# Two-layer hybrid backbone: convolutions issued behind their columns, sums taken from PSUM, first maxima among the last gates, and several loads and tiles moved

## The chip, the cores and the metric

The kernel runs on one core of a Trainium2 chip. A core has TensorE (PE, matrix products, with its weight loads shown as PEld), VectorE (DVE), ScalarE (ACT), GpSimd (POOL) and SyncE (SP, which here only issues transfers). Each engine works through its own queue in order. Transfers (DMA) are issued by SP, ACT or POOL and move data between the memory of the chip and the core's SBUF, by 16 DMA engines. The metric is the device time of one execution in microseconds (us); lower is better.

## The reference, cut to what matters

2048 latent tokens of width 1024, with 256 context tokens, go through two layers. Each layer: RMS norm, modulation by a condition (adaLN), one wide input projection, two mixers side by side, each multiplied by its own SiLU gate, one output projection, and a residual through the modulation's gate. The mixers of the first layer are global grouped attention (8 query heads, 2 key heads, rotary, QK norm) and a Hyena long convolution of order 2; those of the second are windowed attention with a sink and a two-dimensional neighbourhood attention. In short:

```python
# first layer
y_a = global_gqa(q, k, v, k_c, v_c)
y_b = hyena_branch(hu, conv_w, ..., d_skip)
y = jnp.concatenate([y_a * jax.nn.silu(ag), y_b * jax.nn.silu(hg)], axis=-1)
# second layer: windowed_gqa(...) and neighbourhood_attention(...)
# both: x = x + gate * (y @ w_out)
```

Everything is float32.

## The kernel before, in words

**Products.** A float32 operand is split into a high and a low part, and a product is three matmuls (hi*hi, hi*lo, lo*hi; `mm3`, printed in the profile as L221). Weights come as pieces of 256 KB (`wraw`, L241), ACT casts the high part (L242), POOL takes the difference (L243).

**Order.** Blocks of instructions are written in program order, and a planner of the framework places them on the engines by its own simulated times, earlier program order going first when two are ready. Within an engine and within a DMA queue the order is then fixed. Only the matmuls inside the global attention are kept in the order in which they are written (`manual_schedule` for PE). Tiles come from rings of a few buffers; a new tile waits for the last use of the buffer that it takes. Pools that are closed give their place to later pools, so a tile of a new pool can wait for the old pool's last use.

**First layer.** Tokens go in three groups `GRP[0..2]`. For each group: norm, rows of k, v, q (PSUM tile `psA`), columns of `u` for Hyena (`us`, PSUM tile `psB`, stored to `u0`), columns of the gates (`g0`). Between them stand the context's attention and Hyena, and the modulation for the gates and for the second layer: `ada_sum` (L95) adds over weights that are loaded in steps into three PSUM banks of the pool `xp`, tag "x"; transposes (L103) end it. For the last group the order is `us((0, 1)); conv(0); us((2,)); conv(1)`, where `conv(0)` and `conv(1)` are the two parts of `latent_conv`: short convolution on DVE and ACT, transposes, and for part 0 the first transform stage (`hpA`, L668, which uses PSUM tag "x" too). Then come the gate columns, `gate_convs`, the rows of k, v, q, and the last gate columns with the maxima.

**First maxima.** For the softmax the global attention takes a maximum of each query's scores: per unit (4 query blocks x 4 head pairs = 16 units) 40 steps of one matmul `pm` (L892) and one reduction `mx` (L893). Those of the first unit (`first_maxima`, `M0`) run ahead of the attention: `cols` calls `some_maxima` after each of four pairs of columns, seven steps at a time, and 12 steps follow. `max_fin` turns the maxima into a row `mr`, which ACT's queue sends into Q (L945).

**Global attention (`glob_attn`).** 144 batches of two key tiles: scores `pS` (L979, L980), exponential on ACT (`Pt`, L981), values `po` (L998), sums of `Pt` on POOL (`pacc`, L993), and the maxima of the next unit in between (`upto`). `load_k` and `load_q` fetch K and Q. Into the batches `hooks(b)` puts the Hyena steps (110 batches, `hyena_steps`; the first transform's matrix `dA` is loaded by `first_stage`, L661, and cast by ACT, L664), then `out_pools`, then from batch 125 on the first output jobs. A unit's end is `finish` (reciprocal, gate, `finish_y`, which stores the result to `yT` as high and low parts).

**Output jobs (`out_jobs`).** A job takes one tile of 128 tokens and one half of the output columns: weights, the two tiles `oy` of `yT` (L1401), the tile `ox` of x or ctx (L1419), `mm3` into `pso`, the product with the gate (L1425) and the sum with x (L1426). After the attention follow, for each group, residual statistics, norm (transposes `lnpt` L302, `lnh` L305 on ACT), rows and columns of the second layer. In the last group `window_keys` loads the keys and values of the window attention (L1452 to L1454) after the q rows of that attention.

## Time and profile before

| what | value |
|---|---|
| median of 3 runs | 3856.79 us (3853.07 to 3857.14) |
| the profiled execution | 3855.73 us |
| its span | 3854.0 us, 57179 instructions |
| mean granted TensorE clock | 0.975 of 2.4 GHz |
| busy: PE, DVE, ACT, POOL | 94%, 59%, 46%, 45% of the span |
| DMA | 586.23 MB, 152 GB/s over the span |

The span is the time from the first to the last instruction in the trace. "Idle before" in a row is the time in which the engine stood still before that instruction, and the arrow names what ended it. A row's time of start counts from the span's start.

### The profile page before, as it was taken

The page shows a single profiled execution, that of the slowest core. Times are in us where ns is not written, and L with a number is a line of the kernel's source. Part 1 is how long each engine was busy: PE and PEld are TensorE (multiplying, and loading weights), DVE is VectorE, ACT ScalarE, POOL GpSimd, SP SyncE. Part 2 cuts the span into 40 slices and gives each one's busy share as a digit, 9 for nine tenths or more (in the row PEclk, how much of TensorE's full clock was granted, in tenths as well). Part 3 has the DMA queues.
Part 4 walks back from the last instruction along what each step waited for, and adds up shares of the span by engine and source line. Part 5 has one row for each costly group of instructions (what it writes and reads, how often), then busy time and mean ns, then how long its engine had stood idle before and what let it go on. Part 6 is the DMA issues. An engine that isn't in the chain of part 4 may idle for free.

```text
span 3854.0 us, 57179 instructions
## 1 busy us (share of the span) xinstructions
PE 3628.1 (94%) x20112; PEld 2607.1 (68%) x20112; DVE 2284.9 (59%) x4370; ACT 1784.9 (46%) x3480; POOL 1735.3 (45%) x1433
## 2 busy tenths in 40 slices
PE   6999999999779999999989989999999999999999
PEld 2788777666555544555545667778877888888887
DVE  5854862634967765776664348185168167677622
ACT  3644642423526655666452334344144266666610
POOL 1544642222447786777796554353244123222310
PEclk8999999999889999999999999999999999999999
DMA  6343445366666555443253545545566376365365
GB/s 195 118 140 123 133 133 141 114 224 219 203 191 189 172 162 173 123 148 110 91 197 96 146 148 152 164 152 155 157 175 169 118 171 147 90 151 135 113 178 169
DMA packets 537650, 586.23 MB, mean 152 GB/s; under 512 B 70590, under 2 KB 361720, under 8 KB 534290
## 3 DMA queue, kind: packets, MB, share of 16 engines
q1 hardware_dynamic: 521090, 551.10, 48.8%
q10 hardware_dynamic: 13856, 25.18, 1.8%
q0 software_dynamic: 2416, 6.29, 0.6%
q8 instruction: 159, 2.61, 0.3%
q14 instruction: 129, 1.06, 0.1%
HBM read 389.62 MB, written 192.75 MB: 151 GB/s over the span
## 4 chain that ended last, share of the span: by engine, by line
PE 69%; DVE 13%; issue 5%; DMA 5%; ACT 4%; POOL 2%; SPq 1%; ACTq 0%; DVEq 0%; POOLq 0%
PE psB L221 16%; PE pso L221 7%; PE po L998 6%; PE psA L221 5%; PE npt L1580 4%; PE no L1592 4%; PE pS L979 4%; PE pm L892 3%; PE pS L980 3%; PE ns L1561 2%; PE ns L1567 2%; DMA wraw<-in_w_in_dram 2%; PE hpX L806 1%; PE hpC L799 1%; PE hpH L811 1%
## 5 line engine op out<-in xcount | busy, mean ns | idle before, releaser
L243 POOL TENSOR_TENSOR wlo<-wraw,whi 128x512 fp32r<-128x512 f32 x368 | 494.4, 1357 | 784.9 <-ACT whi L242 529.3
L993 POOL TENSOR_TENSOR pacc<-pacc,Pt 128x512 f32<-128x512 f32 x512 | 647.1, 1286 | 191.4 <-ACT Pt L981 189.1
L221 PE MATMUL psB<-hT,whi 128*128 128x512 f32 (+1 forms) x2560 | 659.4, 346 | 3.9 <-DVE bo L341 3.5
L221 PE MATMUL psA<-whi,hT 128*128 128x512 f32 (+1 forms) x1952 | 574.8, 375 | 28.3 <-ACT vt L361 8.4
L893 DVE TENSOR_REDUCE mx<-pm 128x1 f32<-128x512 f32 (+1 forms) x640 | 389.1, 631 | 194.4 <-PE pm L892 190.1
L221 PEld LDWEIGHTS psB<-hT,whi 128*128 128x128 f32 x2560 | 445.1, 190 | 87.0 <-issue 23.9
L981 ACT ACTIVATE Pt<-pS 128x512 f32<-128x512 f32 x576 | 333.0, 597 | 352.5 <-PE pS L980 313.7
L221 PE MATMUL psB<-hT,wlo 128*128 128x512 f32 (+1 forms) x1280 | 433.8, 344 | 0.0
L221 PEld LDWEIGHTS psA<-whi,hT 128*128 128x128 f32 x1952 | 359.0, 194 | 98.7 <-ACT vt L361 11.7
L242 ACT CAST whi<-wraw 128x512 fp32r<-128x512 f32 x368 | 222.2, 618 | 301.4 <-DMA wraw<-in_w_in_dram 119.5
L221 PE MATMUL psA<-wlo,hT 128*128 128x512 f32 (+1 forms) x976 | 358.3, 372 | 0.9 <-POOL wlo L243 0.8
L221 PE MATMUL pso<-whi,oy 128*128 128x512 f32 x1088 | 343.2, 394 | 7.9 <-DMA oy<-yT 7.0
L979 PE MATMUL pS<-Q,K 128*128 128x512 f32 x576 | 330.9, 574 | 15.3 <-ACT Pt L981 14.9
L998 PE MATMUL po<-Pt,V 128*64 128x512 f32 x1152 | 283.0, 613 | 0.0
L221 PEld LDWEIGHTS psB<-hT,wlo 128*128 128x128 f32 x1280 | 242.4, 190 | 41.1 <-issue 10.8
L1580 PE MATMUL npt<-ident,np 128*128 128x128 f32 x1488 | 258.6, 283 | 3.4 <-DVE ggt L1157 1.9
L979 PEld LDWEIGHTS pS<-Q,K 128*128 128x128 f32 x576 | 109.7, 190 | 208.7 <-issue 95.3
L221 PEld LDWEIGHTS pso<-whi,oy 128*128 128x128 f32 x1088 | 205.2, 189 | 59.0 <-DMA oy<-yT 7.0
L980 PE MATMUL pS<-Q,K 65*128 65x512 f32 x576 | 231.3, 402 | 10.9 <-DMA Q<-mr 10.9
L892 PE MATMUL pm<-K,Q 128*128 128x512 f32 x600 | 217.0, 384 | 16.6 <-DVE mx L893 16.5
L221 PE MATMUL pso<-wlo,oy 128*128 128x512 f32 x544 | 213.2, 394 | 1.2 <-POOL wlo L243 1.2
L221 PEld LDWEIGHTS psA<-wlo,hT 128*128 128x128 f32 x976 | 189.9, 195 | 32.4 <-POOL wlo L243 3.1
(345 smaller groups left out, 6490.8 us busy)
## 6 DMA issues: line engine op xcount, KB each, us to landing
wraw<-in_w_in_dram SPq DMA_DIRECT2D x312, 256.0 KB
oy<-yT SPq DMA_DIRECT2D x72, 512.0 KB
qk<-tq SPq DMA_DIRECT2D x50, 512.0 KB
fA<-fev SPq DMA_DIRECT2D x64, 256.0 KB
adaw<-in_w_ada_dram SPq DMA_DIRECT2D x32, 512.0 KB
hxb<-XA SPq DMA_DIRECT2D x64, 256.0 KB
hfb<-fA SPq DMA_DIRECT2D x64, 256.0 KB
XC<-hevc ACTq DMA_DIRECT2D x64, 256.0 KB
```

Of the source, the lines that this page charges most:

```text
L221: T.matmul(ps, a(x, kt), b(y, kt), start=(kt == 0 and n == 0), stop=(kt == 7 and n == 2))
L242: S.copy(hi, w)
L243: G.tensor_tensor(out=lo, in0=w, in1=hi.bitcast(F32), op=ALU.subtract)
L892: T.matmul(pm[:, :n], self.q1[:, h, qt * P:(qt + 1) * P], self.K1(c0, n), start=True, stop=True)
L893: V.tensor_reduce(out=self.mx[:, u, c:c + 1], in_=pm[:, :n], axis=AX.X, op=ALU.max)
L979: T.matmul(s, K1[kv][:, kt * P:(kt + 1) * P], q1[:, h, :], start=True, stop=False)
L980: T.matmul(s, K2[kv][:, kt * P:(kt + 1) * P], q2[:, h, :], start=False, stop=True)
L981: S.activation(pt[:, h, :], s, AF.Exp)
L993: G.tensor_tensor(out=acc[1][:, h], in0=acc[1][:, h], in1=p[:, h], op=ALU.add)
L998: T.matmul(po[64 * h:64 * h + 64, :], vt[:, kt, kv * 64:kv * 64 + 64], p[:, h, :], start=(kt == 0), stop=(kt == 17))
L1580: T.transpose(pt[:, i, :], self.p[h][:, (i0 + i) * P:(i0 + i + 1) * P], ident)
L1592: T.matmul(B["po"][64 * h:64 * h + 64, self.k, :], vt[:, kt, 64 * h:64 * h + 64], self.pT[h, i // 4][:, i % 4, :], start=(i == 0), stop=(i ...
```

## The change

It has eight parts. (1) `us((0,)); conv(0); us((1,)); conv(1); us((2,))` in place of the order above. (2) The 40 maxima of the first unit are called 12, 12, 8 and 8 at a time after the four pairs of the last gate columns, and none after them. (3) `load_k` fetches the first key head in two chunks of columns, 0 to 512 and 512 to 2304. (4) The first transform's matrix of the Hyena steps is loaded at the step `o == 0, k2 == 20`, behind a one-column copy on DVE from that step's tile. (5) In an output job the loads of `oy` stand ahead of the weights; in group 0 the load of x from the third tile on waits for a one-column copy from the x tile two jobs before; the product with the gate is written back to PSUM, and the sum takes it from there. (6) The tiles of the last attention unit's end lie in the ring of `oy` (`last_home`). (7) `window_keys` is called after the v rows of the neighbourhood attention, its loads behind one-column copies from the last v tile. (8) `ev_v` keeps its last tile for that.

```diff
--- before.py
+++ after.py
@@ -347,7 +347,7 @@
 
         def ev_v(self, dst):
             def f(ps, tt):
-                vt = self.rg.tile([P, 512], F32, tag="bo", name="vt", bufs=3)
+                vt = self.late = self.rg.tile([P, 512], F32, tag="bo", name="vt", bufs=3)
                 S.copy(vt, ps)
                 nc.sync.dma_start(dst[tt], vt)
             return f
@@ -362,10 +362,10 @@
                 nc.sync.dma_start(dv[tt], vt)
             return f
 
-    def finish_y(sb, y, ft, t0, n, yT=yT, tags=("yhi", "ylo"), bufs=2, eng=None):
-
-        hi = sb.tile([P, 512], F32R, tag=tags[0], name="yhi", bufs=bufs)
-        lo = sb.tile([P, 512], F32R, tag=tags[1], name="ylo", bufs=bufs)
+    def finish_y(sb, y, ft, t0, n, yT=yT, tags=("yhi", "ylo"), bufs=2, eng=None, home=None):
+
+        hi = home[0] if home else sb.tile([P, 512], F32R, tag=tags[0], name="yhi", bufs=bufs)
+        lo = home[1] if home else sb.tile([P, 512], F32R, tag=tags[1], name="ylo", bufs=bufs)
         S.copy(hi[:, :n], y)
         (eng or V).tensor_tensor(out=lo[:, :n], in0=y, in1=hi[:, :n].bitcast(F32), op=ALU.subtract)
         nc.sync.dma_start(yT[0, ft, :, t0:t0 + n], hi[:, :n].bitcast(F32))
@@ -655,9 +655,11 @@
             V.tensor_tensor(out=y, in0=pt.rearrange("p a b -> p (a b)")[:, :256], in1=gt, op=ALU.mult)
             finish_y(sb, y, 4 + ct, 2048, 256, tags=("cmX", "cmt"), bufs=1)
 
-    def first_stage(sb):
+    def first_stage(sb, late=None):
 
         dA = sb.tile([P, P], F32, tag="dA", name="dA")
+        if late is not None:
+            V.tensor_copy(dA[:, 0:1], late[:, 0:1])
         nc.sync.dma_start(dA, C['dftA'])
         hi = sb.tile([P, P], F32R, tag="dAh", name="dAh")
         lo = sb.tile([P, P], F32R, tag="dAl", name="dAl")
@@ -754,7 +756,6 @@
     def hyena_steps(sb, ps):
 
 
-        dA = first_stage(sb)[1]
         dD = sb.tile([P, 64], F32, tag="hdD", name="hdD")
         nc.sync.dma_start(dD, C['dftD'])
         yb = sb.tile([P, 4, 2048], F32, tag="yb", name="yb")
@@ -765,7 +766,7 @@
 
         def stage_a(o, g, zt):
             pA = [bank("hpA") for _ in range(2)]
-            dA(pA, zt)
+            D["dA"](pA, zt)
             for h in range(2):
                 ev = sb.tile([P, 512], F32, tag="hev", name="hev", bufs=3)
                 S.copy(ev, pA[h])
@@ -799,6 +800,8 @@
             T.matmul(pC, D["dC", o, k2 // 4][:, k2 % 4, :], D.pop(("Y", o, k2)), start=True, stop=True)
             ev = sb.tile([P, 512], F32, tag="hev", name="hevc", bufs=3)
             S.copy(ev, pC)
+            if o == 0 and k2 == 20:
+                D["dA"] = first_stage(sb, ev)[1]
             nc.scalar.dma_start(XC[o, k2].rearrange("r n c -> (r n) c"), ev)
 
         def forward_x(o, k2):
@@ -904,7 +907,7 @@
                 nc.gpsimd.dma_start(ks[-1][64 * s:64 * s + 64, :n].bitcast(F32), k0[0, 0:64, c:c + n])
         return Maxima(lambda c, n: ks[c // 1024][:, c % 1024:c % 1024 + n], q1, mx, bank)
 
-    def glob_attn(sb, ps, hooks, M0):
+    def glob_attn(sb, ps, hooks, M0, last_home):
 
 
         K1, K2 = [None] * 2, [None] * 2
@@ -928,10 +931,13 @@
             return q1, q2, M
 
         def load_k(h, eng=nc.sync):
-            for s in range(2):
-                eng.dma_start(K1[h][64 * s:64 * s + 64].bitcast(F32), k0[h, 0:64, :])
-            G.memset(K2[h][64:65].bitcast(F32), 1.0)
-            eng.dma_start(K2[h][0:64].bitcast(F32), k0[h, 64:128, :])
+            for i, c in enumerate(((0, 512), (512, 2304)) if h == 0 else ((0, 2304),)):
+                c = slice(*c)
+                for s in range(2):
+                    eng.dma_start(K1[h][64 * s:64 * s + 64, c].bitcast(F32), k0[h, 0:64, c])
+                if i == 0:
+                    G.memset(K2[h][64:65].bitcast(F32), 1.0)
+                eng.dma_start(K2[h][0:64, c].bitcast(F32), k0[h, 64:128, c])
 
         def max_fin(q):
             q1, q2, mx = q[0], q[1], q[2].mx
@@ -1000,12 +1006,13 @@
         def finish(n, yo, acc):
 
             qb, hp = units[n]
-            gt = sb.tile([P, 512], F32, tag="agt", name="agt", bufs=1)
+            tail = iter(home[0]) if n == 15 else None
+            gt = next(tail) if tail else sb.tile([P, 512], F32, tag="agt", name="agt", bufs=1)
             nc.sync.dma_start(gt, g0[hp, :, qb * 512:qb * 512 + 512])
             pd = ps.tile([P, 512], F32, tag="m", name="pd", bufs=3)
             for h in range(2):
                 T.matmul(pd[64 * h:64 * h + 64, :], ones[:, 64:P], acc[:, h, :], start=True, stop=True)
-            rec = sb.tile([P, 512], F32, tag="rec", name="rec", bufs=1)
+            rec = next(tail) if tail else sb.tile([P, 512], F32, tag="rec", name="rec", bufs=1)
             S.copy(rec, pd)
 
             def quarter(i):
@@ -1015,11 +1022,12 @@
                 G.tensor_tensor(out=rec, in0=rec, in1=gt, op=ALU.mult)
                 G.tensor_tensor(out=yo, in0=yo, in1=rec, op=ALU.mult)
 
-            return [lambda i=i: quarter(i) for i in range(0, 512, 128)] + [gate, lambda: finish_y(sb, yo, hp, qb * 512, 512, bufs=1, eng=G)]
+            return [lambda i=i: quarter(i) for i in range(0, 512, 128)] + [gate, lambda: finish_y(sb, yo, hp, qb * 512, 512, bufs=1, eng=G, home=home[1] if tail else None)]
 
         batches = [(n, kt) for n in range(16) for kt in range(0, 18, 2)]
         nb = len(batches)
         acc, po, ended, last, pend = {}, {}, {}, None, []
+        home = []
         total = 16 * 41
 
         def upto(b, share):
@@ -1061,7 +1069,9 @@
                 for i in range(2):
                     values(m, ks + i, tiles[i], po[m])
                 if ks == 16:
-                    yo = sb.tile([P, 512], F32, tag="yo", name="yo", bufs=2)
+                    if m == 15:
+                        home[:] = last_home()
+                    yo = home[0].pop() if m == 15 else sb.tile([P, 512], F32, tag="yo", name="yo", bufs=2)
                     S.copy(yo, po.pop(m))
                     ended[b + 2] = m, yo
             if b in ended:
@@ -1316,7 +1326,7 @@
         xs2 = ln_in(GRP[2][0])
         gates()
         ln0(2, xs2)
-        us((0, 1))
+        us((0,))
         ls = s2.enter_context(tc.tile_pool(name="lc", bufs=1))
 
         def conv(part):
@@ -1324,8 +1334,9 @@
                         lambda: sb.tile([P, 1024], F32, tag="lnx", name="zev", bufs=6), (part,))
 
         conv(0)
+        us((1,))
+        conv(1)
         us((2,))
-        conv(1)
         s2.close()
         gates((0,))
         with ExitStack() as s2:
@@ -1334,13 +1345,13 @@
         M0 = first_maxima(lambda: sb.tile([P, 1024], F32R, tag="lnx", name="K1", bufs=6), cp.tile([P, 8, 5], F32, tag="sil", name="mx"),
                           lambda: xp.tile([P, 512], F32, tag="x", name="pm", bufs=3))
 
+        share = [12, 12, 8, 8]
+
         def some_maxima():
-            for _ in range(7):
+            for _ in range(share.pop(0)):
                 M0.step()
 
         pj.cols(2304 + 512, True, g0[4:8], True, some_maxima, (sb, "lnh", 2))
-        while M0.i < 40:
-            M0.step()
     HB = 2
     hy = stH.enter_context(tc.tile_pool(name="hy", bufs=1, **L))
     hyp = stH.enter_context(tc.tile_pool(name="hyp", bufs=1, space=PSUM, **L))
@@ -1391,14 +1402,14 @@
         def job(b, i, tt, mm):
             c = slice(512 * b, 512 * b + 512)
             rg, xo, gl = O0["rg"], O0["xo"], O0["gl"]
+            ty = [xo.tile([P, 8, P], F32R, tag=f"oy{s}", name=f"oy{s}", bufs=2) for s in range(2)]
+            for s in range(2):
+                nc.sync.dma_start(ty[s].bitcast(F32), yT[s, :, :, tt * P:(tt + 1) * P].rearrange("f p t -> p f t"))
             if i == 0 and w_out.get("b") != b:
                 w_out["b"] = b
                 w_out["w"] = load_w(I['w_out'][0][:, c], 512)
             if g == 0 and i == 0:
                 gate_half(gl[:, c], mm("pg"), 0, 0, b)
-            ty = [xo.tile([P, 8, P], F32R, tag=f"oy{s}", name=f"oy{s}", bufs=2) for s in range(2)]
-            for s in range(2):
-                nc.sync.dma_start(ty[s].bitcast(F32), yT[s, :, :, tt * P:(tt + 1) * P].rearrange("f p t -> p f t"))
             gate = gl[:, c]
             if tt == 16:
                 w_out["gc"] = rg.tile([P, 512], F32, tag="bo", name="gc", bufs=3)
@@ -1411,6 +1422,8 @@
             else:
                 if len(xs) == i:
                     xt = xo.tile([P, 1024], F32, tag="lnx", name="ox", bufs=6)
+                    if g == 0 and i > 1:
+                        V.tensor_copy(xt[:, 0:1], xs[i - 2][:, 0:1])
                     if early:
                         for h in range(2):
                             hs = slice(512 * h, 512 * h + 512)
@@ -1421,9 +1434,8 @@
                 x = xs[i][:, c]
             po = mm("pso")
             mm3((po, lambda x, kt: ty[x][:, kt, :], lambda y, kt: w_out["w"][y][kt]))
-            t = rg.tile([P, 512], F32, tag="bo", name="ot", bufs=3)
-            V.tensor_tensor(out=t, in0=po, in1=gate, op=ALU.mult)
-            V.tensor_tensor(out=x, in0=x, in1=t, op=ALU.add)
+            V.tensor_tensor(out=po, in0=po, in1=gate, op=ALU.mult)
+            V.tensor_tensor(out=x, in0=po, in1=x, op=ALU.add)
             if tt < 16:
                 nc.sync.dma_start(rows(x1, tt)[:, c], x)
 
@@ -1437,7 +1449,7 @@
             Proj.stats(pl, b, xs[i:i + nt])
             i += nt
 
-    def window_keys():
+    def window_keys(late):
 
         wm = aw.tile([P, 1152], F32, tag="wm", name="wm")
         nc.sync.dma_start(wm, C['wmask'])
@@ -1447,6 +1459,8 @@
         wk1 = aw.tile([P, 2, 2304], F32R, tag="wk1", name="wk1")
         wk2 = aw.tile([P, 2304], F32R, tag="wk2", name="wk2")
         wvt = aw.tile([P, 18, P], F32, tag="wv", name="wv")
+        for t in (wk1[:, 0, 0:1], wk2[:, 0:1], wvt[:, 0, 0:1]):
+            V.tensor_copy(t, late[:, 0:1])
         for s in range(2):
             r = slice(64 * s, 64 * s + 64)
             nc.sync.dma_start(wk1[r].bitcast(F32), qk1[8:10, 0:64].rearrange("h p t -> p h t"))
@@ -1470,9 +1484,14 @@
             return [], [lambda: j(lambda nm: O0["ps"].tile([P, 512], F32, tag="s2", name=nm, bufs=2))], []
         return [], [], []
 
+    def last_home():
+
+        ty = [O0["xo"].tile([P, 8, P], (F32, F32, F32R)[i], tag=f"oy{i % 2}", name="yl", bufs=2).rearrange("p a b -> p (a b)") for i in range(3)]
+        return [ty[0][:, :512], ty[0][:, 512:], ty[1][:, :512]], (ty[2][:, :512], ty[2][:, 512:])
+
     HB, PB = 2, 5
     with tc.manual_schedule(engines={mybir.EngineType.PE}):
-        glob_attn(ga, gap, hooks, M0)
+        glob_attn(ga, gap, hooks, M0, last_home)
     for j in jobs:
         j(lambda nm: O0["ps"].tile([P, 512], F32, tag="s2", name=nm, bufs=2))
     rg, xo = O0["rg"], O0["xo"]
@@ -1506,11 +1525,11 @@
         pj.load_rope()
         pj.rows(512, 256, True, pj.ev_kv('win_k_norm', qk1[8:10], v1w))
         pj.rows(0, 512, False, pj.ev_q(lambda tt: qk1[0:8][:, :, tt * P:(tt + 1) * P], 'win_q_norm', -0.125, True))
-        if g == 2:
-            wm, sk, wk1, wk2, wvt = window_keys()
         pj.rows(1280, 512, True, pj.ev_q(lambda tt: qk1[18:26][:, :, tt * P:(tt + 1) * P], 'nat_k_norm', 1.0, False))
         pj.rows(768, 512, False, pj.ev_q(lambda tt: qk1[10:18][:, :, tt * P:(tt + 1) * P], 'nat_q_norm', -0.125, False))
         pj.rows(1792, 512, True, pj.ev_v(v1n))
+        if g == 2:
+            wm, sk, wk1, wk2, wvt = window_keys(pj.late)
         for b in range(2):
             pj.cols(2304 + 512 * b, True, g1[4 * b:4 * b + 4], False)
     stC.close()
```

## Rows read from the trace of the kernel before

**Rows 1.** The page's first part: busy us of each engine, its share of the span, and its instructions.

```profile
PE 3628.1 (94%) x20112; PEld 2607.1 (68%) x20112; DVE 2284.9 (59%) x4370; ACT 1784.9 (46%) x3480; POOL 1735.3 (45%) x1433
```

**Rows 2.** The view of waits, PE from 780 to 3100 us. Columns: PE's operation, its line, what it waited for; us in total, times, longest.

```profile
PE pm L892 <- DVE mx L893: 17.8, 15, 4.3
PE pS L979 <- ACT Pt L981: 14.9, 21, 6.2
PE lnpt L302 <- ACT lnh L305: 11.9, 4, 9.9
...
PE pS L980 <- DMA Q<-mr: 10.9, 1, 10.9
...
PE psA L221 <- ACT whi L242: 7.2, 3, 6.8
```

**Rows 3.** The view of stretches: busy us and instructions of PE, weight loads, DVE, ACT and POOL in each stretch, then the granted TensorE clock as a share of 2.4 GHz, the DMA share and GB/s.

```profile
780.00:923.00 143.00, 143.00 (x689) 88.24 (x689) 34.78 (x42) 26.00 (x39) 34.56 (x24) 1.00 0.67 216
923.00:1089.00 166.00, 138.21 (x675) 105.28 (x673) 147.66 (x254) 87.41 (x165) 72.36 (x67) 0.89 0.66 210
1094.00:1128.00 34.00, 30.96 (x159) 23.29 (x157) 28.56 (x52) 5.00 (x10) 9.46 (x10) 0.86 0.71 191
1112.00:1136.00 24.00, 13.43 (x30) 6.40 (x28) 15.91 (x32) 0.84 (x3) 9.46 (x10) 0.63 0.97 245
1984.00:2008.00 24.00, 16.37 (x67) 8.47 (x65) 9.62 (x16) 9.15 (x17) 23.80 (x20) 0.95 1.02 304
2883.00:2910.00 27.00, 18.28 (x74) 13.44 (x73) 19.62 (x30) 8.50 (x17) 17.21 (x13) 0.88 0.91 215
3011.00:3045.00 34.00, 34.00 (x194) 29.66 (x193) 3.40 (x6) 9.76 (x16) 10.77 (x9) 1.00 0.36 111
```

**Rows 4.** The same view for four stretches in which the records show the clock at half (1.2 GHz).

```profile
1118.30:1145.60 27.30, 14.97 (x29) 8.19 (x29) 13.12 (x26) 1.56 (x4) 3.62 (x4) 0.50 0.93 253
2063.80:2067.20 3.40, 3.40 (x10) 2.63 (x10) 1.22 (x3) 0.00 (x0) 0.00 (x0) 0.50 0.19 73
2258.40:2268.60 10.20, 2.73 (x13) 2.73 (x14) 1.46 (x3) 4.18 (x7) 4.87 (x5) 0.50 0.25 85
2903.50:2913.70 10.20, 5.98 (x14) 4.72 (x15) 7.94 (x11) 3.71 (x7) 5.13 (x5) 0.50 0.74 228
```

**Rows 5.** The timeline of PE at the end of the modulation; columns: start in us, busy us, engine, line, operation with output and inputs, count of merged instructions, and in brackets the idle time before them and what ended it.

```profile
920.61 1.05 PE L95 MATMUL ada<-adaw,sil 128*32 128x512 f32 x4
...
922.86 0.60 PE L103 MATMUL adat<-ident,mod 128*128 128x128 f32 x4
923.21 0.47 PE L668 MATMUL hpA<-zst,dAh 128*128 128x512 f32 x1
```

**Rows 6.** The timeline of ACT, same columns: an operand of the first convolution.

```profile
854.16 1.07 ACT L379 CAST zst<-ptz 64x512 fp32r<-64x512 f32 x2
```

**Rows 7.** The view of one tile (the modulation's sums, 850 to 925 us): line, engine, operation, count, shortest/median/longest ns, first and last start in us.

```profile
L95 PE MATMUL ada<-adaw,sil x72: 592/605/617, 849.8 to 921.1; 128*32 128x512 f32 x72
```

**Rows 8.** The timeline of PE around the entry of the global attention.

```profile
1111.61 0.40 PE L221 MATMUL psB<-hT,whi 128*128 128x256 f32 x2
...
1139.35 0.77 PE L980 MATMUL pS<-Q,K 65*128 65x512 f32 x1 [10.88 <-DMA Q<-mr]
1139.91 2.59 PE L892 MATMUL pm<-K,Q 128*128 128x512 f32 x5
```

**Rows 9.** The timeline of DVE there.

```profile
1113.89 13.26 DVE L893 TENSOR_REDUCE mx<-pm 128x1 f32<-128x512 f32 x24
...
1127.99 0.28 DVE L943 CAST mr<-pmt 8x128 fp32r<-8x128 f32 x1 [0.62 <-PE pmt L941]
```

**Rows 10.** The timeline of POOL there.

```profile
1112.42 0.76 POOL L919 DMA_DIRECT2D Q<-q  x1 [19.67 <-PE pm L892]
...
1118.59 0.72 POOL L919 DMA_DIRECT2D Q<-q  x1
```

**Rows 11.** The timeline of ACT there (ACTq is its DMA issue).

```profile
1135.07 0.30 ACT L664 CAST dAh<-dA 128x128 fp32r<-128x128 f32 x1 [22.53 <-DMA dA<-in_dftA_const]
1135.09 1.80 ACTq L945 DMA_DIRECT2D Q<-mr  x2
```

**Rows 12.** The view of one line, L919 from 1110 to 1122 us: its two loads of Q, from issue to landing.

```profile
DMA to landing us min/median/max: 7.2/11.9/16.7
```

**Rows 13.** The timeline of SP's DMA queue inside the attention, at the first output jobs.

```profile
1995.37 3.73 SPq L1419 DMA_DIRECT2D ox<-in_x_dram  x3
```

**Rows 14.** The timeline of ACT there.

```profile
2007.72 0.62 ACT L242 CAST whi<-wraw 128x512 fp32r<-128x512 f32 x1 [6.17 <-DMA wraw<-in_w_out_dram]
```

**Rows 15.** The timeline of DVE at an output job.

```profile
2054.36 0.69 DVE L1425 TENSOR_TENSOR ot<-pso,gl 128x512 f32<-128x512 f32 x1 [4.92 <-PE pso L221]
...
2055.66 7.23 DVE L1426 TENSOR_TENSOR ox<-ox,ot 128x512 f32<-128x512 f32 x1
```

**Rows 16.** The timeline of POOL there.

```profile
2037.61 24.73 POOL L993 TENSOR_TENSOR pacc<-pacc,Pt 128x512 f32<-128x512 f32 x20
```

**Rows 17.** The timeline of ACT at the end of the attention.

```profile
2265.04 1.45 ACT L305 ACTIVATE lnh<-lnpt,gs 128x512 f32<-128x512 f32 x2 [3.77 <-DMA yT<-ylo]
```

**Rows 18.** The timeline of ACT while the window keys are loaded.

```profile
2904.85 0.58 ACT L212 CAST tq<-pt 64x512 fp32r<-64x512 f32 x1 [10.00 <-DMA qk<-tq]
```

**Rows 19.** The view of one line, L780 (one-column copies in the hyena steps during the attention), columns as in rows 7.

```profile
L780 DVE COPY yb<-hY x16: 144/144/154, 1159.3 to 1389.9; 128x1 f32<-128x1 f32 x16
```

## The prediction

> **What bounds the kernel now.** I read the busy shares first: TensorE (PE) is busy for 94% of the span, 3628.1 of 3854.0 us [rows 1]. So a part of this change can pay in two ways only: by closing one of the gaps that make up the other 6%, or by sparing PE the time at half clock (1.2 instead of 2.4 GHz) that the records show after a gap. The second view is the list of PE's waits between 780 and 3100 us [rows 2]; the reader is to see that five of its rows each hold one long single wait (their last number: 10.9, 9.9, 6.8, 6.2 and 4.3 us), and that these five stand at places which the diff touches. The third view is a table of stretches [rows 3]: it tells whether a place is full of PE work, of VectorE (DVE) work or of transfers. The fourth is the same table for the stretches at half clock next to the waits [rows 4].
>
> **The convolutions behind their columns.** First the part named first. Part 0 of the latent convolution is now issued after the first column of u alone, part 1 before the third column. Instructions are the same in number. What would start earlier? In the trace ScalarE (ACT) makes the first convolution operand at 854.16, 69 us before PE uses it at 923.21 [rows 5, 6]. The use follows directly on the last transposes of the modulation, at 922.86 [rows 5]; the convolution's results go into the three PSUM banks that the modulation's sums hold until 921.1 [rows 7]. The columns were therefore not what it waited for, and putting them later cannot bring it forward. After 923 the same work is left: DVE 147.66 of 166 us [rows 3]. I take **0**. Bounds: +10, about half of the 18.3 us in which DVE is idle there; and -8: between 849.8 and 921.1 stand 72 matmuls of the modulation, 18 steps of four [rows 7], one every 71.3/17 = 4.2 us; a step is 1.05 us of PE [rows 5], and one that no column covers leaves 3.1 us open, so two or three uncovered steps.
>
> **First maxima and the entry of the global attention.** 40 maxima remain 40. Now 12, 12, 8 and 8 follow the four pairs of gate columns instead of four times 7 and 12 at the end, so 32 of them compete with the last pair instead of 21. Before, 24 reductions run in one row from 1113.89 for 13.26 us, after the last column matmul at 1111.61 [rows 8, 9]. DVE is idle for 34 - 28.56 = 5.4 us of 1094:1128 [rows 3]; filling it ends the maxima at best 4.6 us earlier. But the loads of Q and K wait for the last column matmul (1112.42 [rows 10]); seven more maxima ahead of it, at 0.26 us (five at half clock took 2.59 [rows 8]), put it 1.8 us later, and three more load pieces on POOL's queue at 0.7 us (as 1112.42 and 1118.59) are another 2.1 us. The stretch 1112:1136 is bound by transfers (DMA share 0.97, 245 GB/s [rows 3]). The vector of maxima is ready at 1127.99 + 0.28 = 1128.3 [rows 9]; its transfer into Q stands on ACT's queue behind the cast of the transforms' matrix, which waited 22.53 us for its load [rows 11], and PE got it 10.9 us late [rows 2]. With the matrix held back to the 20th step it could land at about 1128.3 + 4.3 (1135.09 to 1139.35, where PE's wait ended [rows 8, 11]) = 1132.5. What is late next: five maxima of the second unit follow the first scores on PE (1139.91 [rows 8]), and they need that unit's Q, issued 1118.59 and landed up to 16.7 us later, 1135.3 [rows 10, 12]; the two delays make it 1139.2 if none of them is absorbed. So the gain is 1139.9 less 1135.3 to 1139.2, 4.6 to 0.7, and I take **+3**. Bounds: +7 (10.9 less the 4.3 of the transfer); -2, if Q of the second unit is later still. The half clock from 1118.3 on [rows 4] stays, since the gap only shrinks.
>
> The matrix itself, one load, a cast and a difference, moves among the hyena steps with one 1-column copy. Its load waits for that copy and ACT's cast for the load; behind the cast stand exponentials, and PE behind them. I take **-0.5**; bounds 0 and -4, what the small transfer at 1135.09 took to PE in full traffic.
>
> **Output jobs inside the attention.** (1) Four of six loads of x or ctx, 512 KB each, are held until the sum two jobs before. Before, they are issued in one go (three in 3.73 us from 1995.37 [rows 13]) while the DMA share is 1.02 at 304 GB/s [rows 3], and ACT then waits 6.17 us at 2007.72 for weights queued behind them [rows 14]; exponentials stand behind ACT's cast, and PE waits 6.2 [rows 2]. 2 MB at 304 GB/s are 6.9 us, more than the wait. But the held loads come back among the next weights. Between 0 and 9 (the wait and what the half clock after it costs) I take two thirds of the wait, **+4**. (2) The sum is now taken from PSUM. DVE's sum of two SBUF tiles took 7.23 us at 2055.66, the product from PSUM just before it 0.69 us [rows 15], both inside one unbroken run of 20 POOL additions from 2037.61 for 24.73 us [rows 16]. PE's gap behind the reduction was 4.3 [rows 2], and 3.40 us then ran at half clock [rows 4], 1.7 of them lost: 6.0 in all. I take **+5.5**, bounds 3.5 and 6. The product written back to PSUM has the form of the 0.69 us row; nothing else on the path is dearer. (3) The loads of y ahead of the weights inside a job: 0, the weights of a half column are wanted only after both.
>
> [...]
>
> **The last unit's tiles from another ring.** ACT's first normalised tile waits until 2265.04 for the store of the last attention tile [rows 17], because it takes that tile's place; PE is idle 9.9 us [rows 2] and 2.73 us of work then run at half clock [rows 4]. With the last tiles in the ring of y, the wait's object is gone: 9.9 + 1.4 = 11.3 at most. Late next are the loads of constants and weights that SP issues behind that store, and the y loads of the next group, whose ring is now held longer. I take **+7**, bounds 2 and 10.
>
> **Window keys later.** The loads of window keys, 4.7 MB, leave a stretch with DMA share 0.91 [rows 3]: ACT waits 10.00 us for a tile of q whose store is on its way [rows 18], and PE 6.8 us behind ACT's weight cast [rows 2]; 5.98 us of PE at half clock follow [rows 4], 3.0 lost: 9.8 at most. They go to where PE is full (34.00 of 34) and the DMA share is 0.36 [rows 3]. The weights that are loaded there belong to the next gate column, 34 us on; 4.7 MB at 215 GB/s are 22 us. If they went ahead of weights that are needed at once, 6 us of it would come back. Three 1-column copies on DVE cost under 0.5 us, and DVE has 30 idle. I take **+7**, bounds 0 and 10.
>
> **Sum.** 0 + 3 - 0.5 + 4 + 5.5 + 7 + 7 = 26 us. The profiled execution took 3855.73 us (span 3854.0); 3855.7 - 26 = 3829.7. The median of the runs is 3856.79, 1.1 above it: **3831**.
>
> **Rivals.** *The next transfer fills the gaps.* Four of the five waits lie in or behind stretches where transfers fill most of the time (0.97, 1.02, 0.91 [rows 3]); a later load can end at the same time whatever went ahead of it. Only the PSUM sum, 5.5, and 3 of the last unit's 7 would stay: 3848. Against: the share around 2260 is 0.25 [rows 4], and the keys go to a stretch at 0.36. Chance 0.17. *The convolutions do start early.* If the planner found other banks or times for them in 780:923, where DVE is busy for 34.78 of 143 us [rows 3], the stretch after would fall from DVE's 166 to near PE's 138 + waits, about 20 us more: 3811. Against: the three banks. Chance 0.07. *Slower.* The convolution's operations stand earlier in the program, so on DVE and ACT, which go in order, they may be placed ahead of evacuations of the second and third columns, and wait there for the banks; column matmuls then stop, and the modulation goes on at the pace of its loads, 3.1 us open per step. From 10 uncovered steps on (31 us) this outweighs the 26; with 13 of the 18 (40 us) it is 3871. For: PE is full there only because columns cover it. Against: 143.00 of 143 before, with ample operands. Chance 0.11. *Held copies block.* If each of the four copies of part (1) stood behind POOL's additions as the 7.23 us sum did and cost PE its 6.0, 24 us would be given back: 3855. Against: 16 one-column copies during the attention took 144 to 154 ns, so none was blocked [rows 19]. [...] Chance 0.05.
>
> **How the numbers follow.** Forecast 0.60, all of it faster. A measurement here can tell about 0.2%, 7.7 us: faster ends at 3849, slower begins at 3864.5. Of the first rival 0.07 is faster and 0.10 the same; the second is faster; the third slower; the fourth the same. Faster 0.60 + 0.07 + 0.07 = 0.74, same 0.15, slower 0.11. The bounds of the terms added up give 52 and -8.5 us, both improbable; half-way out, and to take in the first and fourth rivals, the range is 3804 to 3858, which leaves out the third and part of the second.
>
> **What would show it.** Right: no sum from 7 us on DVE; ACT's matrix cast away from 1135; no PE gap over 3 us before the first normalised tile's transposes and behind the keys' old place; loads of keys after the last v row; the convolution's first matmul still directly behind the modulation's transposes. Wrong: PE gaps between 850 and 921; a convolution matmul ahead of 923; new waits of PE for weights after 3011 or near 2270; the second unit's maxima waiting for Q past 1140.

## The result

The changed kernel takes **3820.1 us** (median of four runs, 3816.99 to 3825.89) against 3855.57 us before (four runs): a ratio of 0.991, 95% interval 0.9893 to 0.9928. Some 35 us are gone; the forecast was 3831, 26 us. A second set of runs of the same kernel gave 3819.65 us (0.9901, 0.9887 to 0.9914). The profiled execution of the first set is the slowest of its runs, 3825.89 us with a span of 3824.1; a second profiled execution has a span of 3814.1. So one profile tells where the time went, but not the total to better than about 10 us.

**The profile after.** PE's list of waits from 780 to 3070 us, columns as in [rows 2]:

```profile
PE pm L895 <- DVE mx L896: 12.6, 11, 2.4
...
PE ptz L739 <- DVE uc L728: 9.5, 2, 5.0
PE pso L221 <- DMA oy<-yT: 8.9, 10, 3.9
...
PE pS L985 <- ACT Pt L987: 8.0, 18, 2.3
...
PE pS L986 <- DMA Q<-mr: 6.8, 1, 6.8
...
PE lnpt L302 <- ACT lnh L305: 3.7, 6, 1.3
```

Of the five long single waits (10.9, 9.9, 6.8, 6.2, 4.3) only the first is left, shortened to 6.8. The wait for the weights' cast is gone: from 2840 to 2990 us, around the old place of the window keys, PE never waits longer than 1.2 us. The normalised transposes wait 0.7 us where it was 9.9. A sixth long wait stood in the same list of the kernel before, in the convolutions' stretch at 972.72 us, in a row that [rows 2] leaves out:

```profile
PE ptz L737 <- DVE uc L726: 10.8, 2, 6.3
```

The change left it: its longest wait is 5.0 us in this profile and 6.3 in the second. The timeline of PE there, and of PE at the end of the modulation (answers to [rows 5]):

```profile
2239.22 1.53 PE L302 MATMUL lnpt<-ident,ox 128*128 128x128 f32 x12 [0.68 <-ACT yl L1016]
2241.46 1.33 PE L302 MATMUL lnpt<-ident,ox 128*128 128x128 f32 x8 [0.71 <-ACT lnh L305]
2245.15 0.58 PE L221 MATMUL psA<-whi,hT 128*128 128x256 f32 x1 [2.36 <-DVE hT L306]
```

```profile
924.76 0.60 PE L103 MATMUL adat<-ident,mod 128*128 128x128 f32 x4
925.11 0.47 PE L670 MATMUL hpA<-zst,dAh 128*128 128x512 f32 x1
```

Twelve transposes run at 2239.22, eight more 0.71 us after them, and the first product of the second layer waits 2.36 us for VectorE. The convolution's first matmul at 925.11 still follows directly on the modulation's transposes. DVE's and ACT's timeline at the entry of the attention (answers to [rows 9, 11]), then the lines of the sum from PSUM and of the held copies (shortest, median, longest ns; answers to [rows 15, 19]):

```profile
1115.35 13.25 DVE L896 TENSOR_REDUCE mx<-pm 128x1 f32<-128x512 f32 x24
...
1129.44 0.28 DVE L949 CAST mr<-pmt 8x128 fp32r<-8x128 f32 x1 [0.62 <-PE pmt L947]
```

```profile
1129.81 2.01 ACTq L951 DMA_DIRECT2D Q<-mr  x2
```

```profile
L1438 DVE TENSOR_TENSOR ox<-pso,ox x30: 679/691/692, 2048.7 to 2803.4; 128x512 f32<-128x512 f32 x30
```

```profile
L1426 DVE COPY ox<-ox x4: 142/142/142, 2050.5 to 2080.9; 128x1 f32<-128x1 f32 x4
```

The 24 reductions in one row are there as before, to 0.01 us. The row of maxima is sent as soon as it is ready, at 1129.81. No sum takes over 0.69 us, and no held copy over 0.14. The stretches at the old and the new place of the window keys, and at the first output jobs (columns as in [rows 3]):

```profile
1984.00:2008.00 24.00, 22.50 (x90) 10.84 (x86) 11.01 (x18) 13.25 (x24) 21.99 (x19) 1.00 0.79 231
2870.00:2900.00 30.00, 28.18 (x128) 21.56 (x129) 27.68 (x51) 10.95 (x23) 18.13 (x15) 1.00 0.45 127
2981.00:3015.00 34.00, 33.64 (x192) 29.25 (x191) 3.42 (x9) 7.84 (x14) 6.42 (x5) 1.00 0.93 234
```

In the window of the first output jobs PE is busy for 22.50 of 24 us where it was 16.37, and the DMA share fell from 1.02 to 0.79 (the same times of the span, in which the changed kernel is some us further on). At the old place of the keys the share fell from 0.91 to 0.45; at the new place it is 0.93, and PE is busy for 33.64 of 34 us: the keys cost PE at most 0.36 us there.

**Where the time went.** The same instruction of PE stands in every profile, so the difference of its start in two profiles tells how far one is ahead. The table gives for each stretch how much PE gained (-) or lost (+) on the profile of before; it is worked out from the starts of the instructions that bound a stretch (last modulation transpose, last maximum of the first unit, sixth of the second, scores 800, 1000 and 1150 of 1152, normalised transposes 192, last one, first window score). The third column is the span over the eleven profiles of the variants below, without those that undo a part that acts in that stretch (for the first output jobs these are experiments 5, 7 and 9 to 11).

```
stretch (us, before)                first   second   others           forecast
start to 923                         +1.9    -2.6    -2.7 to +5.9     -
923 to 1126   convolutions, maxima   -0.5    -0.2    -1.1 to -0.1      0
1126 to 1143  entry of attention     -4.1    -4.7    -4.7 to -4.0     -2.5
1143 to 1880  Hyena steps             0.0    -1.3    -5.3 to +0.5     -
1880 to 2047  first output jobs      -4.3    -5.7    -6.0 to -2.1     -4
2047 to 2248  sums                   -8.3    -8.4    -8.4 to -7.4     -5.5
2248 to 2507  last unit's tiles     -11.2   -11.6    -12.7 to -10.1   -7
2507 to 2848  jobs, second layer     +2.3    -1.4    -0.5 to +6.1     -
2848 to 3080  window keys            -6.1    -4.6    -6.4 to -4.7     -7
3080 to end                          +0.4    +0.7    -1.4 to +1.5     -
```

The first row is hardly work of the change: at 785 us, ahead of the first edited block, the variants already stand from 2.6 us ahead of before to 4.4 behind, and by the modulation's end they differ among themselves by 8.6 us. What makes this difference is not shown. The fourth row holds clock that falls or not behind the same short gaps (last section); the eighth holds such clock too (3.41 us at half clock before, 6.83 in the first profile), and waits for loads of y, which differ from 5.3 to 9.5 us.

### The profile page after: what moved, and what is told of

The parts are those of the page before. It is cut to its first block, busy times and chain, and to the rows that moved or that the text cites. A ratio compares the mean times of both kernels' runs of the same rounds, so it can differ in the third digit from the quotient of the medians.

```text
span 3824.1 us, 57213 instructions
## 1 busy us (share of the span) xinstructions
PE 3631.6 (95%) x20112; PEld 2606.3 (68%) x20112; DVE 2268.3 (59%) x4378; ACT 1785.5 (47%) x3480; POOL 1736.2 (45%) x1436
## 4 chain that ended last, share of the span: by engine, by line
PE 69%; DVE 14%; issue 5%; DMA 5%; ACT 4%; POOL 2%; SPq 1%; ACTq 0%; DVEq 0%; POOLq 0%
PE psB L221 16%; PE pso L221 8%; PE po L1004 7%; PE npt L1599 4%; PE pS L985 4%; PE no L1611 4%; PE psA L221 4%; PE pS L986 3%; PE pm L895 3%; PE ns L1580 2%; PE ns L1586 2%; DMA wraw<-in_w_in_dram 2%; PE hpX L809 1%; DVE tq L213 1%; PE hpC L800 1%
```

## The experiments

All are edits of the changed kernel. Each has four or five timed runs; the time is the median, the ratio that to the kernel before, run beside it. Intervals are 0.0025 to 0.0035 wide, 5 to 7 us to each side, so only the trace can tell of anything smaller, and that from one profiled execution each.

**1. The changed kernel again.** No edit.

> The changed kernel once more, unedited. Both theories: the convolutions' first matmul again directly behind the modulation's transposes, 24 reductions of the first unit's maxima in one row after the last gate column. Theory of additive parts: the runs give 0.990 to 0.993 of before, and the loss of about 4 us that the first profile shows between 1945 and 1970 us (half clock with the same work on every engine) is chance, so it is away or elsewhere in this profile. Rival, that the change itself brings this loss (a later phase of every transfer): it stands at the same place, within 5 us.

Measured: 3819.65 us, 0.9901. The convolution and the 24 reductions stood as expected. The loss near 1955 us came back at the same place, 4.1 us in both profiles and in every variant that loads K in chunks: the rival was right, it is no chance. ACT's timeline in the first profile, then in that of experiment 7, which has no chunks:

```profile
1955.42 0.62 ACT L369 CAST yhi<-yb 128x512 fp32r<-128x512 f32 x1 [1.88 <-DMA yT<-ylo]
1958.77 0.62 ACT L369 CAST yhi<-yb 128x512 fp32r<-128x512 f32 x1 [2.73 <-DVE ylo L370]
1960.87 0.62 ACT L369 CAST yhi<-yb 128x512 fp32r<-128x512 f32 x1 [1.48 <-DMA yT<-ylo]
1961.39 1.08 ACT L987 ACTIVATE Pt<-pS 128x512 f32<-128x512 f32 x2
```

```profile
1957.60 0.62 ACT L369 CAST yhi<-yb 128x512 fp32r<-128x512 f32 x1 [1.84 <-DMA yT<-ylo]
1959.43 1.30 ACT L987 ACTIVATE Pt<-pS 128x512 f32<-128x512 f32 x2 [1.21 <-PE pS L986]
1960.97 0.62 ACT L369 CAST yhi<-yb 128x512 fp32r<-128x512 f32 x1 [0.25 <-DVE ylo L370]
1961.50 1.08 ACT L987 ACTIVATE Pt<-pS 128x512 f32<-128x512 f32 x2
```

In the first, three casts of Hyena's results stand in a row, each waiting for a store or for VectorE (1.88, 2.73, 1.48 us), and the exponentials come after the third; PE stands 2.3 us until 1962.03 and then runs at half clock until 1968.43; in the second profile it stands 3.9 us, and its granted clock from 1950 to 1970 is 0.91 of full speed. In the second the planner put two exponentials after each of the casts shown.

**2. The sum from SBUF again.**

```diff
-            V.tensor_tensor(out=po, in0=po, in1=gate, op=ALU.mult)
-            V.tensor_tensor(out=x, in0=po, in1=x, op=ALU.add)
+            t = rg.tile([P, 512], F32, tag="bo", name="ot", bufs=3)
+            V.tensor_tensor(out=t, in0=po, in1=gate, op=ALU.mult)
+            V.tensor_tensor(out=x, in0=x, in1=t, op=ALU.add)
```

> The changed kernel with the output jobs' sum taken from SBUF tiles again. Theory of additive parts: the first sum meets a run of additions on POOL and takes 4 to 8 us instead of 0.69; a reduction behind it is late, PE stands 2 to 5 us, half clock follows: 4 to 7 us slower than the changed kernel between 2040 and 2075 us of the span, the rest as before. Rival, that the sum was only in the way of a load that ends at the same time: under 1 us slower at the end of the attention.

Measured: 3830.24 us, 0.9929 (0.9916 to 0.9941); the stretch 2047 to 2248 gains 3.5 us on before instead of 8.3, so the sum is worth 4.8 there. The runs say 10 us. In the stretch before, which ends 9 us ahead of the first sum, this kernel loses another 2.2 to 3.6 us; these and the rest of the 10 are not explained. Lines of the sum, of POOL, and of the unit's end:

```profile
L1439 DVE TENSOR_TENSOR ox<-ox,ot x30: 679/692/4437, 2049.5 to 2807.2; 128x512 f32<-128x512 f32 x30
```

```profile
2049.48 4.44 DVE L1439 TENSOR_TENSOR ox<-ox,ot 128x512 f32<-128x512 f32 x1
```

```profile
2031.00 22.37 POOL L999 TENSOR_TENSOR pacc<-pacc,Pt 128x512 f32<-128x512 f32 x18
```

```profile
2054.58 0.38 PE L895 MATMUL pm<-K,Q 128*128 128x256 f32 x1 [1.55 <-DVE mx L896]
```

```profile
2119.29 1.72 DVE L1439 TENSOR_TENSOR ox<-ox,ot 128x512 f32<-128x512 f32 x1
```

```profile
2122.23 0.37 PE L947 MATMUL pmt<-ident,nm 128*8 128x128 f32 x1 [2.29 <-DVE nm L945]
```

The first sum takes 4.44 us and ends at 2053.92, 0.5 us after POOL's row of additions (2031.00 + 22.37 = 2053.37). PE waits 1.55 us behind it, and against the changed kernel 1.9 us are lost there, 0.35 more than the wait, where the theory had 4 to 7. Three more sums took 1.66, 1.73 and 1.72 us. The last of them, at 2119.29, makes the unit's last maximum late: PE waits 2.29 us where the changed kernel waits 1.25, runs at half clock for 3.41 us after it, and most of the other 2.9 us are lost there. The mechanism of the theory holds, its place and size only in part; the rival does not hold. The two profiles of before and after show the same: of the 18 sums from SBUF between 2055 and 2250 us of the kernel before, the four that began while POOL added (2055.66, 2105.73, 2116.21, 2129.87) took 7.23, 1.66, 1.73 and 1.72 us, and the 14 that began while POOL stood took 0.68 or 0.69; in the changed kernel the four sums from PSUM that began while POOL added (2048.71, 2092.53, 2103.01, 2116.28) took 0.68 each.

**3. The last unit's tiles in their own rings.**

```diff
-                    if m == 15:
-                        home[:] = last_home()
-                    yo = home[0].pop() if m == 15 else sb.tile([P, 512], ...)
+                    yo = sb.tile([P, 512], ...)
...
-            tail = iter(home[0]) if n == 15 else None
+            tail = None
```

> The changed kernel with the last attention unit's tiles in their own rings again. Theory of additive parts: PE's gap of about 10 us before the fifth to sixteenth normalised transposes comes back, and 7 to 11 us are lost by 2500 us of the span. Rival, next transfer fills: the weights of the second layer are late in either kernel, and less than 3 us are lost by 2500 us.

Measured: 3831.2 us, 0.9934 (0.9922 to 0.9947), 11 us slower than the changed kernel; from 2248 to 2507 it gains 0.5 us on before instead of 11.2. PE's waits from 2225 to 2300 us:

```profile
PE lnpt L302 <- ACT lnh L305: 9.7, 1, 9.7
```

The wait of 9.7 us is back. The theory holds, at the upper end.

**4. The window keys at the old place.** Without the three copies, too.

```diff
+        if g == 2:
+            wm, sk, wk1, wk2, wvt = window_keys(None)
         pj.rows(1280, 512, True, pj.ev_q(...))
...
-        if g == 2:
-            wm, sk, wk1, wk2, wvt = window_keys(pj.late)
```

> The changed kernel with the window keys loaded at their old place, after the q rows of the window attention. Theory of additive parts: a gap of PE of 5 to 8 us behind ACT's weight cast comes back around 2875 us, half clock behind it, 7 to 10 us lost by the start of the second layer's attention. Rival, next transfer fills: the stores and weights of that stretch are late in either kernel, under 3 us lost.

Measured: 3824.61 us, 0.9915 (0.9901 to 0.9929), about 5 us slower. From 2848 to 3080 it gains 0.1 us on before instead of 4.6 to 6.4. ACT and PE there:

```profile
2870.00 0.58 ACT L212 CAST tq<-pt 64x512 fp32r<-64x512 f32 x1 [9.87 <-DMA qk<-tq]
```

```profile
PE psA L221 <- ACT whi L242: 6.7, 1, 6.7
```

The waits of 10.00 and 6.8 us of before come back as 9.87 and 6.7. The theory holds on the mechanism; the worth in the trace, 4.5 to 6.0, lies under the 7 to 10 named.

**5. x not held.**

```diff
-                    if g == 0 and i > 1:
-                        V.tensor_copy(xt[:, 0:1], xs[i - 2][:, 0:1])
```

> The changed kernel without the copies that hold the loads of x back (the loads of y still ahead of the weights). Theory of additive parts: ACT waits again about 6 us for weights queued behind the loads of x, PE about as long, and 4 to 9 us are lost between 1960 and 2030 us of the span. Rival, that putting y ahead of the weights or chance brought the gain there: under 2 us lost.

Measured: 3821.41 us, 0.9907. No wait of ACT for weights over 0.8 us from 2000 to 2025, and 1880 to 2047 gains 7.8 us, 2.1 to 3.5 more than the changed kernel and as much as the two without chunks (7.7 in experiments 7 and 9). The theory fell. The rival has the size right, under 2 us lost; that y ahead of the weights brought the gain is not borne out by experiment 10.

**6. The matrix at the beginning again.**

```diff
+        dA0 = first_stage(sb)[1]
...
-            D["dA"](pA, zt)
+            dA0(pA, zt)
...
-            if o == 0 and k2 == 20:
-                D["dA"] = first_stage(sb, ev)[1]
```

> The changed kernel with the transforms' matrix loaded at the beginning of the attention again. Theory of additive parts: the row of maxima is sent only after ACT's cast of the matrix, near 1135 instead of 1130 us, and PE's first wait of the attention is 10 to 11 instead of 6.2 to 6.8 us: the whole gain at the entry (4.1 to 4.7 us) is the matrix. Rival, the chunks of K: the wait stays at 6 to 7 us. On the loss of 4 us between 1945 and 1962 us, which three more profiles of variants repeated at the same place: if holding the matrix shifts the planner's order there, PE's gap of 2 to 4 us behind three casts in a row on ACT is away in this kernel and 4 us come back.

Measured: 3819.01 us, 0.9902. PE's first wait is 6.5 us and the entry gains 4.4: the matrix alone is not the gain. The loss near 1955 stayed as well. ACT's timeline shows why:

```profile
1128.48 2.04 ACTq L950 DMA_DIRECT2D Q<-mr  x2
1135.39 0.30 ACT L666 CAST dAh<-dA 128x128 fp32r<-128x128 f32 x1 [22.73 <-DMA dA<-in_dftA_const]
```

The cast still waits for its load until 1135.39, but the planner now has the sending of the row ahead of it.

**7. The first key head in whole pieces.**

```diff
-            for i, c in enumerate(((0, 512), (512, 2304)) if h == 0 else ((0, 2304),)):
+            for i, c in enumerate(((0, 2304),)):
```

> The changed kernel with the first key head of the attention loaded in one piece per row block again. Theory: the chunks are worth nothing or cost up to 1.5 us, since the first score does not wait for K in any profile: PE's first wait of 6.2 to 6.8 us stays or is up to 1.5 us shorter. Rival: 2 to 4 us lost at the entry. The planner's order near 1950 us: if the chunks shift it, the 4 us come back here.

Measured: 3822.74 us, 0.991. The wait is 6.2 us and the entry gains 4.6: the chunks bring nothing there. Near 1955 the loss of 4.1 us is away (0.0), and the three casts are no longer in a row (the second fence of experiment 1): it is the chunks that shift the planner's order there. From 1880 to 2047 the kernel gains 7.7 us, 2.0 to 3.4 more than the changed one; the runs do not tell it.

**8. Old order of columns, convolutions and maxima.**

```diff
-        us((0,)) ... conv(0); us((1,)); conv(1); us((2,))
+        us((0, 1)) ... conv(0); us((2,)); conv(1)
...
-            for _ in range(share.pop(0)):
+            for _ in range(7):
...
+        while M0.i < 40:
+            M0.step()
```

> The changed kernel with the columns of u and the convolutions in the old order and the maxima seven at a time with 12 at the end again. Theory: no difference: the first convolution's matmul directly behind the modulation's last transposes, 24 reductions in one row after the last gate column; within 1 us between 785 and 1127 us of the span against the other profiles, after taking off where each stands at 785. Rival, that these parts bring 3 us or more each: they show there. The planner's order near 1950 us: if these parts shift it, 4 us come back.

Measured: 3821.22 us, 0.9904. From 923 to 1126 it gains 0.9 us on before where the others gain 0.1 to 1.1: no difference. Its 24 reductions start at 1114.27 and take 13.25 us. The convolutions' new place and the maxima's new share, two of the parts in the title, brought nothing that shows.

**9. Both parts at the entry undone.** Experiments 6 and 7 in one kernel.

> The changed kernel with both the matrix loaded at the beginning of the attention and the first key head in whole pieces. Theory: what counts at the entry is the order on ACT's queue alone. With either of the two parts the planner puts the sending of the maxima's row ahead of the matrix's cast, without both it puts it behind: the row goes near 1135, PE's first wait is 10 to 11 us, 4 to 5 us are lost at the entry. At 1950 us, without the chunks, the three casts in a row are away and 4 us come back, so the total stays within 2 us of the changed kernel. Rival: the wait stays at 6 to 7 us, since something else (the new share of the maxima) brought the gain.

Measured: 3822.93 us, 0.9909. ACT's timeline and PE's wait:

```profile
1130.73 0.30 ACT L666 CAST dAh<-dA 128x128 fp32r<-128x128 f32 x1 [22.03 <-DMA hdB<-in_dftB_const]
1130.76 1.80 ACTq L950 DMA_DIRECT2D Q<-mr  x2
```

```profile
PE pS L985 <- DMA Q<-mr: 9.5, 1, 9.5
```

The cast is ahead of the sending again, PE waits 9.5 us, and the entry gains 1.4 instead of 4.0 to 4.7: 2.6 to 3.3 lost, less than the 4 to 5 expected: against before, the row is sent 6.3 instead of 6.8 us after it is ready (1124.43 and 1128.27), and reaches PE 3.35 instead of 4.26 us after that. The three casts near 1955 are away (0.0 there). The theory holds on both orders.

**10. y behind the weights, and neither y nor x changed.** The second is this edit with that of experiment 5.

```diff
-            ty = [...]; the two loads of ty
             if i == 0 and w_out.get("b") != b:
                 w_out["w"] = load_w(...)
             if g == 0 and i == 0:
                 gate_half(...)
+            ty = [...]; the two loads of ty
```

> The changed kernel with the loads of y behind the weights of a job again, the loads of x still held. Theory: either of the two parts shifts the casts of the first weights on ACT behind more exponentials; with the hold alone no wait over 3 us comes back between 1960 and 2030 us, under 2 us lost. Rival: y ahead of the weights is the part that brought the gain: PE waits 4 to 7 us again near 2000.

> The changed kernel with neither the hold of x nor y ahead of the weights. Theory: with both away a wait of ACT for weights with exponentials behind it comes back, PE stands 4 to 7 us near 2000 and runs at half clock after it: 5 to 9 us lost between 1962 and 2046 us. Rival: the gain there is due to the other parts (the planner's order after the chunks), and under 2 us are lost.

Measured: 3820.29 us (0.9904) and 3820.58 us (0.9906). With y behind alone, 1880 to 2047 gains 5.7 us, as the second profile of the changed kernel does. With both undone it gains 2.7. PE's waits there:

```profile
PE pS L985 <- ACT Pt L987: 6.0, 4, 2.1
```

The longest wait is 2.1 us, that of the three casts; the 6.2 us of before did not come back. Of the 5 to 9 us expected, 1.6 to 3.0 were lost against the first and second profile of the changed kernel (4.3 and 5.7). Even these do not lie at the weights. Up to score 970 this kernel has gained 6.7 us, the changed one 3.3 and 4.7; behind that it loses 4 us, most of it at a short wait with half clock after it:

```profile
2023.51 0.79 PE L985 MATMUL pS<-Q,K 128*128 128x512 f32 x1 [1.77 <-ACT Pt L987]
```

```profile
2023.35:2030.18 6.83, 6.67 (x15) 2.80 (x16) 1.38 (x2) 1.78 (x4) 6.83 (x7) 0.50 0.00 0
```

So neither the trace nor the runs show a worth of the two parts. The first weights are issued at 1974.75 here and at 1984.09 before. This kernel is 9.0 us ahead of before at score 800 and only 4.9 at score 900, where PE lost 4.1 us; the transfers kept their time (1974.75 + 9.0 = 1983.8), so they come 4 us earlier as PE counts. That the loss near 1955 so took most of the old wait away is argued from this, not tried: a kernel with neither these parts nor the chunks was not run.

**11. Without the four parts that brought nothing alone.** Experiments 5, 7 and 8 in one kernel: kept are the matrix held back, y first, the sums from PSUM, the tiles in the ring of y, and the late keys.

> The changed kernel without the four parts that brought nothing alone: columns and convolutions in the old order, the maxima's old share, the first key head in whole pieces, x not held. Kept: the matrix held back, y ahead of the weights, sums from PSUM, the last unit's tiles in the ring of y, the keys late. Theory: entry wait 6 to 7 us, no gap of 2 to 4 us behind three casts near 1955, no wait of 4 us or more near 2000: as fast as the changed kernel or up to 4 us faster. Rival: the four parts carry something in the sum, and it is 3 us or more slower.

Measured: 3823.45 us, 0.9908 (0.9892 to 0.9925). Neither theory nor rival is decided: 3 to 4 us above the changed kernel's medians, within the interval. From 1126 us to the end its trace gains 34.2 us on before, between the two profiles of the changed kernel (31.3 and 37.0). Near 1955 it loses 1.9 us, though the casts are apart; PE's longest wait near 2000 is 3.2 us, half of that of before, with y ahead of the weights as the one part left there. No version was found that beats the changed kernel by more than the runs can tell.

## Why the prediction was right, and where its steps were not

The direction and the range were right, and so was the reading that bore them: PE was full, and long single waits at the places of the change could be taken away. The five waits are 38 of the 226 us in which PE stood; a sixth of 6.3 us, in the convolutions' stretch, was left out of the list and was not touched by the change. The mechanisms of the sums, of the last unit's tiles and of the keys went as written. 35 us were gained for 26, by the tiles (4 more than the term) and the sums (3 more) above all. The range does not follow from its own words: half-way out, and widened for the two rivals, its lower end would be near 3818, not 3804, which is the sum of all upper bounds. The result, 3820.1, lies inside either.

**Convolutions, 0.** Right, and the first convolution matmul follows directly on the modulation's transposes in both orders, so the columns did not hold it. That it was the banks which did is argued from the kernel; no run freed them.

**First maxima.** The step "32 of them compete with the last pair instead of 21" led nowhere: not one maximum moved, DVE idles before the last columns as it did, and so the 1.8 us of delay that I charged for it were not paid either.

**Entry, +3 less 0.5.** The size was near: 4.0 to 4.7, inside the bounds. The mechanism was the one written, the row no longer stands behind the matrix's cast on ACT's queue, and holding the matrix back is enough for it (experiment 7). What the prediction did not have is that the matrix need not move: with the chunks alone the planner puts the sending ahead of the cast (experiment 6), and only with neither is it behind (experiment 9). The transfer of the row took 6.9 us from issue to PE's start, not 4.3 (1129.81 to 1136.67), and the second unit's Q landed near 1136 too (issued 1121.60, 14.2 us), so it does not show which of the two would have been late alone. The 0.5 to 4 us for the matrix in the Hyena steps were not seen: ACT's cast at 1315.0 waits 0.3 us for its load.

**First output jobs, +4.** The net was 4.3 and 5.7, but that it came near the term is luck. Holding x, which should have brought it, brought nothing that shows; the net is made up of the old wait that went (in every variant, or was halved as in experiment 11; which part took it away is not shown) and of a loss of 4.1 us near 1955 that no part of the prediction had: the chunks made the planner put three casts in a row on ACT. That the planner may rearrange engines hundreds of us behind an edit should have been a term with its own bounds.

**Sums, +5.5.** Against before the stretch gained 8.3. 6.3 of them lie at the first sum, the stall of 7.23, where the prediction had 6.0 at most; the other 2.0 come after it, most of them at the unit's end, where before had sums of 1.66 to 1.73 us that the prediction did not count. Experiment 2 shows the mechanism, but of its 4.8 only 1.9 lie at its stall of 4.44; the stall of 1.72, with the unit's last maximum behind it, cost more.

**Last unit's tiles, +7.** 11.2 and 11.6, outside its bounds of 2 to 10 and near the 11.3 that it named as the most. The failed step is the deduction for "late next": ACT does wait 4.5 us for weights, at 2246.55, but PE's next waits are 2.4 and 1.5 us only.

**Keys, +7.** 4.6 to 6.4, inside the bounds. The new place hid the loads (PE busy for 33.64 of 34 us there). Less than the 9.8 of the wait and its half clock came back, since other waits grew: PE's waits in the stretch fell from 11.9 to 7.3 and 8.8 us only, with 3.2 us for VectorE's `qn` where it was 1.1.

**Rivals.** "The next transfer fills the gaps": no, experiments 3 and 4. The convolutions did not start early; nothing was slower; the held copies took 142 ns. None was blocked, as in [rows 19]. By the trace, the undone parts cost 4.8 (sums), 10.7 to 11.1 (tiles) and 4.5 to 6.0 us (keys); by the runs 10, 11 and 5. The sums' 10 against 4.8 stays open. The rest of the 35 is the entry and the output jobs, which the runs do not separate.

## What to carry to other kernels

A long single wait of the full engine, with the name of what ended it, was worth here up to its length and the half clock behind it: the tiles (11.2 and 11.6 of 11.3 us) and the first sum (6.3 of 6.0) gave back all of that, the keys (4.6 to 6.4 of 9.8) and the entry (4.0 to 4.7 of a wait of 10.9) about half. Take away the object of the wait (the buffer, the queue place, the SBUF operand) and test it by putting that one object back. Where a planner fixes the order of the other engines, compare the order of each queue, not only the edited lines: here one wait was shortened because an instruction no longer stood ahead of another, which either of two edits causes, and another came 840 us behind the edit that caused it. A new order in the program need not move anything: the convolutions and the maxima ran as before.

## What the runs showed of the hardware

Gaps of one length cost different amounts of clock here. Before, PE stood 2.30 us until 1435.29 and ran at half clock for 3.41 us; after, it stood 2.31 us at the same instruction and ran at half clock for 6.82. The second profile of the changed kernel, the same program, stood 2.31 us there and ran at half clock for 3.41. The three stretches, before, after and second profile (columns as in [rows 3]):

```profile
1435.74:1439.15 3.41, 3.41 (x12) 1.56 (x12) 2.21 (x5) 1.14 (x3) 3.23 (x4) 0.50 0.49 145
```

```profile
1432.55:1439.37 6.82, 6.82 (x19) 2.38 (x18) 1.58 (x3) 2.10 (x4) 4.53 (x4) 0.50 0.61 216
```

```profile
1426.91:1430.32 3.41, 3.41 (x11) 1.47 (x11) 2.13 (x5) 1.27 (x3) 3.33 (x4) 0.50 0.45 138
```

That is 1.7 us of difference, half of the 3.41 more at half clock, from nothing in the program. Such pieces make most of the spread between the profiles from 1143 to 1880 us: there the first profile runs at half clock for 19.0 us in all and that of experiment 4 for 6.8, and the latter gains 5.3 us more.
